# Filter norms and skip terms of a long convolution as rows instead of columns

## The chip, the core and the metric

The kernel runs on one core of a Trainium2 chip. A core has a matrix engine (TensorE, PE; its weight loads are shown apart as PEld), a vector engine (VectorE, DVE), a scalar engine (ScalarE, ACT), GpSimd (POOL), and a queue processor (SyncE, SP) that here issues most of the DMAs. They share an on-chip memory of 128 partitions (SBUF) and the accumulators of TensorE (PSUM). Each engine works through its own list of instructions in order and waits on semaphores for the others. The metric is the device time of one execution in microseconds (us).

## The reference

One layer of an encoder block on x of 2048 positions by 1024 channels, float32: an RMS norm and a projection to a Fourier group (512 channels) and three Hyena groups (3 x 512); a two-dimensional FFT over the Fourier group; an order-2 gated long convolution over the Hyena groups; an output projection, and an MLP. What bears on the change is the filters of the long convolution and how they are used:

```
def implicit_filters(l, w0, b0, w_inner, b_inner, freq, w_out):
    ...                                     # small MLP over the positions: h
    h = (h @ w_out).reshape(l, HYENA_ORDER, N_DIRECTIONS, HYENA_WIDTH)
    h = h * decay[:, None, None, :]
    k = concatenate([h_fwd[:1] + h_bwd[:1], h_fwd[1:], zeros, h_bwd[1:][::-1]])
    return k * lax.rsqrt(jnp.sum(k * k, axis=0, keepdims=True) + EPS)

def fft_long_conv(u, k_freq, d):
    y = jnp.fft.irfft(jnp.fft.rfft(u, n=2 * l) * k_freq)[:l]
    return y + u * d
...
    for n, gate in enumerate((x1, x2)):
        z = gate * fft_long_conv(z, k_freq[:, n], long_d[n])
```

Each of the 2 x 512 filters has 4096 taps and is scaled by one number, the inverse root of its sum of squares plus EPS. The skip term u * d of the convolution is the same as adding d to tap 0 of the scaled filter.

## The kernel before, in words

Products that need full float32 are made of three faster ones (`mm3`, lines 211 to 213, on operands split into a high and a low part by `split`, line 197). The stages follow each other: a first pass of the input projection (to 224 us), a second pass of it with the short convolution (224 to 411), the filters and the Fourier group (411 to 583), then the long convolutions, the output projection and the MLP.

`filters` works on 8 units. Unit i is the channel tile ct = i // 2 (128 channels) and the order n = i % 2 of the convolution. A unit's filter tile `k` has the taps over partitions and columns, the 128 channels inside the columns; tap 0 is partition 0. A unit goes through these parts, spread over a loop of 44 steps, in which several units overlap:

- steps 4u to 4u+3, `generate`: 32 small products (line 596) make a quarter of the taps in a PSUM buffer (`pair`, two buffers in turn, shared with `stage1`), VectorE multiplies it by the decay into `k` (line 601), ScalarE squares it (line 615), GpSimd adds the squares up in `acc` (lines 619 to 622). After the first quarter two taps are added (lines 610 to 612).
- step 4u+5, `normalise` and `scales`: a product sums `acc` over the partitions (`psum_k`, line 627), so that each channel's sum of squares stands in one partition of a 128x1 tile; VectorE adds EPS (`vk`), ScalarE takes the root (line 631), VectorE the reciprocal (line 222) and one Newton step (lines 225 to 227): `sc`. The filter itself is not scaled. Instead tap 0 gets d times the root of the sum (`dk`, line 639, from `vk`, `sc` and `longd`), and the product of the scales of both orders goes into `norms`, which later multiplies the gated input (line 740).
- step 4u+6, `skip`: `dk` is a column, tap 0 of `k` a row over channels. Two products turn the one round and add the other in PSUM (`pdk`, lines 650 and 651), and ScalarE copies the sum back to `k` (line 652). For n = 1 the column of both scales (`both`) is made a diagonal by ScalarE (line 645), a product with ones puts it in all partitions as a row (`pdiag`, line 655), and ScalarE copies it to `norms`.
- from step 4u+7, `stage1` (line 668, transposed out of PSUM by VectorE, line 672) and from 4u+12 `stage2` (line 678, copied by ScalarE, stored by DMA): the filter's spectrum.

`long_d` is loaded as 8 rows of 128, and at the start of `filters` turned into columns (`plongd`, line 556; `longd`, line 557).

The order of TensorE's instructions in this stage is the order of the code, kept by queue-order dependencies (`ordered`, `behind`). The order on the other engines, and of the DMAs on SP's queue, comes from a scheduler, which interleaves all of the program: the steps of the Fourier group (`pf`, lines 508 to 528, and `row`, lines 539 and 540) stand among the first 11 steps, and the weight differences of the MLP (`f`, lines 1484 to 1487, for `second_weights`) among the second pass of the projection.

`rsqrt` has two forms, for a tile of one column and for a wider one:

```
nc.vector.reciprocal(r, s)
if v.shape[1] == 1:
    ...  # 3 tensor_scalar, L225 to L227
nc.vector.tensor_mul(q, r, r)            # L229
nc.vector.tensor_mul(q, q, v)            # L230
nc.vector.tensor_scalar(out=q, in0=q, scalar1=-0.5, scalar2=1.5, ...)  # L231
nc.vector.tensor_mul(q, r, q)            # L232
```

Of the kernel before, what the change touches and what calls it, by code (L numbers as in the profile page):

```python
# [10 lines left out]
F32 = mybir.dt.float32  # L11
# [3 lines left out]
ALU = mybir.AluOpType  # L15

EPS = 1e-5
# [110 lines left out]
P = 128  # L128
# [6 lines left out]
def hybrid_block(ctx: ExitStack, tc: tile.TileContext, A, out):  # L135
    nc = tc.nc
# [36 lines left out]
    def pa(nm):  # L173
        banks["n"] += 1
        pl, tag = (ps, "a") if banks["two"] or banks["n"] % 2 else (banks["other"], "b")
        return pl.tile([P, 512], F32, tag=tag, name=nm, bufs=4)
# [371 lines left out]
            yield  # L548


    def filters(ctx, tp, fp, gp, zp, zzs, norms, emb, wo, e1k, f2, dk8, tabs, fourier_steps):


        longd = fp.tile([P, 16], F32, tag="longd", name="longd")[:, 0:8]
        p = pa("plongd")
        nc.tensor.transpose(p[:, 0:8], dk8, ident[0:8, 0:8])
        nc.scalar.copy(longd, p[:, 0:8])

        class Unit:
            def __init__(self, i):  # L560
# [63 lines left out]
            def normalise(self):  # L624

                p = pa("psum_k")
                ordered(nc.tensor.matmul(p[:, 0:1], lhsT=self.acc[:, 0, :], rhs=ones[:, 0:1], start=True, stop=True))
                self.v = fp.tile([P, 1], F32, tag="vk", name="vk", bufs=2)
                nc.vector.tensor_scalar(out=self.v, in0=p[:, 0:1], scalar1=EPS, scalar2=None, op0=ALU.add)
                self.root = fp.tile([P, 1], F32, tag="sq_k", name="sq_k", bufs=2)  # L630
                nc.scalar.sqrt(self.root, self.v)

            def scales(self):

                v = self.v
                self.sc = rsqrt(v, fp, "k", 8, self.root)
                self.dk = fp.tile([P, 1], F32, tag="dk", name="dk", bufs=2)
                j = 4 * self.n + self.ct
                nc.vector.tensor_scalar(out=self.dk, in0=v, scalar1=self.sc, scalar2=longd[:, j : j + 1], op0=ALU.mult, op1=ALU.mult)
                if self.n:  # L640

                    both = fp.tile([P, 1], F32, tag="both", name="both", bufs=2)
                    nc.vector.tensor_scalar(out=both, in0=self.sc, scalar1=units[self.i - 1].sc, scalar2=None, op0=ALU.mult)
                    self.diag = fp.tile([P, 128], F32, tag="diag", name="diag")
                    nc.scalar.mul(self.diag, ident, both)

            def skip(self):

                p, zero = pa("pdk")[0:1, 0:128], self.k[0:1, :, 0, :]
                ordered(nc.tensor.matmul(p, lhsT=self.dk, rhs=ident, start=True, stop=False))  # L650
                ordered(nc.tensor.matmul(p, lhsT=ones[0:1, 0:1], rhs=zero, start=False, stop=True))
                nc.scalar.copy(zero, p.rearrange("p (c j) -> p c j", c=8))
                if self.n:
                    p = pa("pdiag")
                    ordered(nc.tensor.matmul(p[:, 0:128], lhsT=ones, rhs=self.diag, start=True, stop=True))
                    nc.scalar.copy(norms[:, self.ct], p[:, 0:128])

            def stage1(self, r):
                if r == 0:
# [41 lines left out]
        for step in range(44):  # L701
# [12 lines left out]
                units[u].stage2(2 * q)  # L714
                units[u].stage2(2 * q + 1)
            u, q = divmod(step - 5, 4)
            if 0 <= u < 8 and q < 2:
                (units[u].normalise, units[u].skip)[q]()
            u, k = divmod(step, 4)
            if 0 < step < 32:  # L720
                units[u].generate(k)
# [738 lines left out]
    with pool("ip") as ip, pool("cp1") as cp1:  # L1460
# [67 lines left out]
        e1f, e1k, turn, gy, dk8, e1z, wo, emb, f2 = got  # L1528
    norms = early.enter_context(pool("norms", "right")).tile([P, 4, 128], F32, tag="norms", name="norms")
    with pool("filters") as fp:  # L1530
        zzs, f2h = [], []
        gp = early.enter_context(pool("gk", "right"))
        spx = early.enter_context(ExitStack())
        psum("psd")
        with pool("fourier", "right") as fo:
            ffs.insert(0, load(fo, "ff0", [P, 1, 2, P], A["ff"][:, 0:1]))
            filt = filters(spx, tp, fp, gp, zp, zzs, norms, emb, wo, e1k, f2, dk8, f2h, fourier(fo, uf, e1f, ffs))
            next(filt)
        run(filt)
        psum("psb2")  # L1540
# [73 lines left out]
```

## Time and profile before

| | |
|---|---|
| runs | 2239.90, 2241.47, 2246.95 us; median 2241.47 |
| profiled execution | 2239.05 us, of which the span of the trace 2237.3 |
| mean granted clock of TensorE | 0.996 |
| TensorE busy | 2192.4 us (98%) |
| VectorE busy | 1468.4 us (66%) |
| ScalarE busy | 1072.4 us (48%) |
| GpSimd busy | 762.3 us (34%) |
| stage of the filters | 411 to 583 us |

A row of the timeline gives the start in us, the duration in us, the engine, the line of the kernel, the operation, output<-inputs, tile sizes, how many like instructions were put together (x), and in brackets how long the engine was idle before and what ended that. A group row gives the count, the busy time in us, the mean of one in ns, then the idle time before and what ended most of it. The spans on POOL are rough.

### The profile page before, as it was taken

To read this page: it belongs to the slowest core of one execution; us is meant where nothing else is said; L and a number is where in the kernel's file an instruction comes from. 1 tells how busy PE (TensorE), PEld (TensorE's weight loads), DVE (VectorE), ACT (ScalarE), POOL (GpSimd) and SP (SyncE) were. 2 spreads that over 40 slices of the span, in tenths; PEclk is the share of its full clock that TensorE was granted. 3 is DMA by queue.
4 is the path that set the end of the run, shared out by engine and by line. 5 is a ranking of instruction groups with operands and counts; after the bars stand their busy time and mean duration, and the time that the engine had idled before them with its cause. 6 is when DMAs were issued, how large, how long until landed. Compare 5 with 4: busy or idle time off the path is not lost. (4 is left out here: it accounts for less than half of the span.)

```text
span 2237.3 us, 34489 instructions
## 1 busy us (share of the span) xinstructions
PE 2192.4 (98%) x12881; PEld 1793.3 (80%) x12881; DVE 1468.4 (66%) x2192; ACT 1072.4 (48%) x1783; POOL 762.3 (34%) x576
## 2 busy tenths in 40 slices
PE   8999899999999999999999999999999999999998
PEld 6888778676888778887888878888888888888886
DVE  6998767776788764467444464444476666866667
ACT  6554211355555654546555565555443333533333
POOL 3444323465366511327555446555200000000000
PEclk9999999999999999999999999999999999999999
DMA  8534797569998756586444465444498756866631
GB/s 266 177 134 159 268 335 295 191 218 350 314 306 260 234 161 183 169 265 211 155 156 155 155 238 167 153 146 151 160 381 297 242 188 197 305 194 189 199 111 76
DMA packets 287001, 475.95 MB, mean 213 GB/s; under 512 B 17573, under 2 KB 131439, under 8 KB 282097
## 3 DMA queue, kind: packets, MB, share of 16 engines
q1 hardware_dynamic: 280593, 458.22, 61.5%
q10 hardware_dynamic: 6240, 15.53, 2.1%
q8 instruction: 101, 1.65, 0.3%
q14 instruction: 67, 0.55, 0.1%
HBM read 312.51 MB, written 168.00 MB: 215 GB/s over the span
## 5 line engine op out<-in xcount | busy, mean ns | idle before, releaser
L197 ACT CAST qahm<-ra 128x1024 fp32r<-128x1024 f32 x110 | 115.9, 1053 | 345.0 <-PE p2u L212 171.7
L197 DVE TENSOR_TENSOR qalm<-ra,qahm 128x1024 fp32r<-128x1024 f32 x110 | 134.7, 1224 | 153.4 <-ACT qahm L197 151.7
L1379 POOL TENSOR_TENSOR acc<-acc,gfin 128x512 f32<-128x512 f32 x4 | 5.1, 1282 | 630.2 <-DMA out<-acc 624.4
L212 PE MATMUL pu<-wl,xh 128*128 128x512 f32 x512 | 201.9, 394 | 6.9 <-DVE wl L197 6.5
L211 PE MATMUL pu<-wh,xh 128*128 128x512 f32 x512 | 204.9, 400 | 2.6 <-ACT wh L201 2.6
L213 PE MATMUL pu<-wh,xl 128*128 128x512 f32 x512 | 201.8, 394 | 2.7 <-DVE xl L197 2.7
L212 PE MATMUL p2u<-qblm,qahm 128*128 128x512 f32 x504 | 196.1, 389 | 0.0
L211 PE MATMUL p2u<-qbhm,qahm 128*128 128x512 f32 x504 | 195.8, 389 | 0.0
L213 PE MATMUL p2u<-qbhm,qalm 128*128 128x512 f32 x504 | 195.8, 389 | 0.0
L197 DVE TENSOR_TENSOR qblm<-rb,qbhm 128x1024 fp32r<-128x1024 f32 x110 | 134.0, 1218 | 2.2 <-ACT qbhm L197 2.2
L421 POOL TENSOR_TENSOR acc<-acc,cw 128x512 f32<-128x512 f32 x45 | 60.9, 1354 | 197.5 <-DVE acc L398 194.3
L212 PEld LDWEIGHTS pu<-wl,xh 128*128 128x128 f32 x512 | 97.4, 190 | 28.8 <-DVE wl L197 6.9
L197 ACT CAST ahm<-s 128x512 fp32r<-128x512 f32 x120 | 74.4, 621 | 94.1 <-PE p1v L212 54.8
L197 ACT CAST qbhm<-rb 128x1024 fp32r<-128x1024 f32 x110 | 115.3, 1048 | 4.4 <-DMA rb<-in_w_fc 2.9
L213 PEld LDWEIGHTS pu<-wh,xl 128*128 128x128 f32 x512 | 97.2, 190 | 24.4 <-DVE xl L197 4.1
L211 PEld LDWEIGHTS pu<-wh,xh 128*128 128x128 f32 x512 | 97.4, 190 | 23.8 <-ACT wh L201 3.5
L197 POOL TENSOR_TENSOR alm<-W,ahm 128x512 fp32r<-128x512 f32 x60 | 83.3, 1390 | 86.8 <-ACT ahm L197 86.8
L211 PEld LDWEIGHTS p2u<-qbhm,qahm 128*128 128x128 f32 x504 | 94.6, 188 | 20.1 <-issue 0.3
L213 PEld LDWEIGHTS p2u<-qbhm,qalm 128*128 128x128 f32 x504 | 94.6, 188 | 19.8
L212 PEld LDWEIGHTS p2u<-qblm,qahm 128*128 128x128 f32 x504 | 94.6, 188 | 19.5
L1155 DVE TENSOR_TENSOR c<-p1v,ku 128x512 f32<-128x512 f32 x64 | 44.2, 690 | 89.9 <-ACT ku L1225 51.2
L197 POOL TENSOR_TENSOR alm<-s,ahm 128x512 fp32r<-128x512 f32 x60 | 92.2, 1537 | 29.6 <-ACT ahm L197 29.6
(379 smaller groups left out, 6148.9 us busy)
## 6 DMA issues: line engine op xcount, KB each, us to landing
ks<-spec SPq DMA_DIRECT2D x64, 512.0 KB
W<-in_w_fc SPq DMA_DIRECT2D x64, 512.0 KB
rb<-td SPq DMA_DIRECT2D x64, 512.0 KB
ra<-a1m SPq DMA_DIRECT2D x56, 512.0 KB
ra<-a0m SPq DMA_DIRECT2D x54, 512.0 KB
rb<-in_w_fc SPq DMA_DIRECT2D x46, 512.0 KB
f<-in_w_fc SPq DMA_DIRECT2D x16, 1024.0 KB
td<-f SPq DMA_DIRECT2D x16, 1024.0 KB
```

The lines of the kernel that those rows point to most:

```text
L197: return nc.scalar.copy(hi, src), eng.tensor_sub(lo, src, hi)
L211: a = nc.tensor.matmul(o, lhsT=lh, rhs=rh, start=start, stop=False, skip_group_check=more)
L212: nc.tensor.matmul(o, lhsT=lh, rhs=rl, start=False, stop=False, skip_group_check=more)
L213: return a, nc.tensor.matmul(o, lhsT=ll, rhs=rh, start=False, stop=stop, skip_group_check=more)
L421: nc.gpsimd.tensor_add(m1, m1, cw[:, 3, :])
L1155: read["DVE"] = nc.vector.tensor_add(c, p, other)
L1379: nc.gpsimd.tensor_mul(acc[i][:, c], acc[i][:, c], gfin[:, c])
```

## The change

The sums stand as rows from the start. `psum_k` becomes a product with ones on the other side: it puts every channel's sum in all 128 partitions, 128 columns wide. EPS, root, reciprocal and Newton step are done on these 128x128 tiles (the wide form of `rsqrt`). Tap 0 of `k` is in partition 0, where the row of sums stands too, so `dk` is made there by two products of 1x128 and added to `k` by VectorE; `norms` is the product of two 128x128 tiles. `skip`, `both`, `diag`, `pdk`, `pdiag`, `longd` and `plongd` go. `long_d` is loaded as one row per unit in one partition, at the start of `filters`.

```diff
-    def filters(ctx, tp, fp, gp, zp, zzs, norms, emb, wo, e1k, f2, dk8, tabs, fourier_steps):
-        longd = fp.tile([P, 16], F32, tag="longd", name="longd")[:, 0:8]
-        p = pa("plongd")
-        nc.tensor.transpose(p[:, 0:8], dk8, ident[0:8, 0:8])
-        nc.scalar.copy(longd, p[:, 0:8])
+    def filters(ctx, tp, fp, gp, zp, zzs, norms, emb, wo, e1k, f2, tabs, fourier_steps):
+        dk8 = load(fp, "dk8", [1, 8, 128], A["long_d"])
...
             def normalise(self):
                 p = pa("psum_k")
-                ordered(nc.tensor.matmul(p[:, 0:1], lhsT=self.acc[:, 0, :], rhs=ones[:, 0:1], start=True, stop=True))
-                self.v = fp.tile([P, 1], F32, tag="vk", name="vk", bufs=2)
-                nc.vector.tensor_scalar(out=self.v, in0=p[:, 0:1], scalar1=EPS, scalar2=None, op0=ALU.add)
-                self.root = fp.tile([P, 1], F32, tag="sq_k", name="sq_k", bufs=2)
+                ordered(nc.tensor.matmul(p[:, 0:128], lhsT=ones, rhs=self.acc[:, 0, :], start=True, stop=True))
+                self.v = fp.tile([P, 128], F32, tag="vk", name="vk")
+                nc.vector.tensor_scalar(out=self.v, in0=p[:, 0:128], scalar1=EPS, scalar2=None, op0=ALU.add)
+                self.root = fp.tile([P, 128], F32, tag="sq_k", name="sq_k")
                 nc.scalar.sqrt(self.root, self.v)
             def scales(self):
-                v = self.v
-                self.sc = rsqrt(v, fp, "k", 8, self.root)
-                self.dk = fp.tile([P, 1], F32, tag="dk", name="dk", bufs=2)
-                j = 4 * self.n + self.ct
-                nc.vector.tensor_scalar(out=self.dk, in0=v, scalar1=self.sc, scalar2=longd[:, j : j + 1], op0=ALU.mult, op1=ALU.mult)
+                self.sc = rsqrt(self.v, fp, "k", 2, self.root)
+                dk, zero = self.root[0:1], self.k[0:1, :, 0, :]
+                nc.vector.tensor_mul(dk, self.v[0:1], self.sc[0:1])
+                nc.vector.tensor_mul(dk, dk, dk8[:, self.i])
+                nc.vector.tensor_add(zero, zero, dk.rearrange("p (c j) -> p c j", c=8))
                 if self.n:
-                    both = fp.tile([P, 1], F32, tag="both", name="both", bufs=2)
-                    nc.vector.tensor_scalar(out=both, in0=self.sc, scalar1=units[self.i - 1].sc, scalar2=None, op0=ALU.mult)
-                    self.diag = fp.tile([P, 128], F32, tag="diag", name="diag")
-                    nc.scalar.mul(self.diag, ident, both)
-            def skip(self):
-                p, zero = pa("pdk")[0:1, 0:128], self.k[0:1, :, 0, :]
-                ordered(nc.tensor.matmul(p, lhsT=self.dk, rhs=ident, start=True, stop=False))
-                ordered(nc.tensor.matmul(p, lhsT=ones[0:1, 0:1], rhs=zero, start=False, stop=True))
-                nc.scalar.copy(zero, p.rearrange("p (c j) -> p c j", c=8))
-                if self.n:
-                    p = pa("pdiag")
-                    ordered(nc.tensor.matmul(p[:, 0:128], lhsT=ones, rhs=self.diag, start=True, stop=True))
-                    nc.scalar.copy(norms[:, self.ct], p[:, 0:128])
+                    nc.vector.tensor_mul(norms[:, self.ct], self.sc, units[self.i - 1].sc)
...
-            if 0 <= u < 8 and q < 2:
-                (units[u].normalise, units[u].skip)[q]()
+            if 0 <= u < 8 and q == 0:
+                units[u].normalise()
...
-                got.append(cpool.tile([8, 128], F32, tag="dk8", name="dk8"))
-                for n in range(2):
-                    nc.sync.dma_start(got[-1][4 * n : 4 * n + 4, :], A["long_d"].rearrange("a (c n) j -> n (a c) j", n=2)[n])
```

Three places show what stands on the engines now. In the changed kernel the lines behind `rsqrt` have other numbers (601 becomes 598, 672 becomes 654, 668 becomes 650, 678 becomes 660, 596 becomes 593, 1484 to 1487 become 1466 to 1469). First VectorE (DVE), unit 4 (n = 0), from its sum to the second product by the decay behind it; before:

```order
L629 TENSOR_SCALAR vk<-psum_k 128x1
L222 RECIPROCAL rc_k<-sq_k 128x1
L225 TENSOR_SCALAR nw_k<-rc_k,vk 128x1
L226 TENSOR_SCALAR nw_k<-nw_k 128x1
L227 TENSOR_SCALAR nw_k<-nw_k,rc_k 128x1
L639 TENSOR_SCALAR dk<-vk,nw_k,longd 128x1
L601 TENSOR_TENSOR k<-pk,dec 128x8x8x16
L672 STREAM_TRANSPOSE Gk<-pk_5171 128x8x2x32 x2
L601 TENSOR_TENSOR k<-pk,dec_4723 128x8x8x16
```

And on the same engine at the same place in the changed kernel:

```order
L626 TENSOR_SCALAR vk<-psum_k 128x128
L222 RECIPROCAL rc_k<-sq_k 128x128
L229 TENSOR_TENSOR nw_k<-rc_k 128x128
L230 TENSOR_TENSOR nw_k<-nw_k,vk 128x128
L231 TENSOR_SCALAR nw_k<-nw_k 128x128
L598 TENSOR_TENSOR k<-pk,dec 128x8x8x16
L232 TENSOR_TENSOR nw_k<-rc_k,nw_k 128x128
L634 TENSOR_TENSOR sq_k<-vk,nw_k 1x128
L635 TENSOR_TENSOR sq_k<-sq_k,dk_3611 1x128
L654 STREAM_TRANSPOSE Gk<-pk_5146 128x8x2x32 x2
L636 TENSOR_TENSOR k<-k,sq_k 1x8x16
L598 TENSOR_TENSOR k<-pk,dec_4706 128x8x8x16
```

The operations became 128 columns wide, and three more of them stand ahead of the transpose; the add into tap 0 stands behind it. With n = 1 the product for `norms` (line 638) stands ahead of the transpose too. Second, TensorE (PE) at the same place, before:

```order
L627 MATMUL psum_k<-ones,acc 128x1
L596 MATMUL pk<-wo,emb 32x128 x32
L668 MATMUL pk_5171<-k,e1k 32x512 x8
L678 MATMUL pk_5190<-Gk,f_2585 128x128 x4
L678 MATMUL pk_5197<-Gk,f_2585 128x128 x4
L650 MATMUL pdk<-ident,dk 1x128
L651 MATMUL pdk<-k,ones 1x128
L596 MATMUL pk<-wo,emb 32x128 x32
L668 MATMUL pk_5248<-k,e1k 32x512 x8
```

And TensorE in the changed kernel:

```order
L624 MATMUL psum_k<-acc,ones 128x128
L593 MATMUL pk<-wo,emb 32x128 x32
L650 MATMUL pk_5146<-k,e1k 32x512 x8
L660 MATMUL pk_5167<-Gk,f_2582 128x128 x4
L660 MATMUL pk_5174<-Gk,f_2582 128x128 x4
L593 MATMUL pk<-wo,emb 32x128 x32
L650 MATMUL pk_5221<-k,e1k 32x512 x8
```

The two `pdk` products are gone; the order is the same otherwise. Third, VectorE in one of the blocks of the second projection pass (`xl` is the low part of a block of x that TensorE multiplies by, `f` the weight differences), before:

```order
L398 SCALAR_TENSOR_TENSOR m_3134<-pu_3103,nw_s,cw_2366 128x512
L197 TENSOR_TENSOR xl<-xc,xh 128x1024
L417 TENSOR_TENSOR acc<-acc,m_3134 128x512
L1484 TENSOR_TENSOR f_2585<-f_2585 128x512
L1485 TENSOR_TENSOR f_2585<-f_2585 128x512
```

And VectorE in the same block of the changed kernel:

```order
L398 SCALAR_TENSOR_TENSOR m_3131<-pu_3100,nw_s,cw_2366 128x512
L1466 TENSOR_TENSOR f_2582<-f_2582 128x512
L417 TENSOR_TENSOR acc<-acc,m_3131 128x512
L1467 TENSOR_TENSOR f_2582<-f_2582 128x512
L197 TENSOR_TENSOR xl<-xc,xh 128x1024
L1468 TENSOR_TENSOR f_2582<-f_2582 128x512
L1469 TENSOR_TENSOR f_2582<-f_2582 128x512
```

Two weight differences stand ahead of the split of x here; in another block it is the other way round. On SP's queue, with one load fewer, some loads of this pass stand up to 15 places earlier.

More of the change, by code (lines that the diff above doesn't have):

```diff
@@ L1527, in hybrid_block @@
         run(project(ip, fx, (None, cp1), (-1, 0), uf), tables())
-        e1f, e1k, turn, gy, dk8, e1z, wo, emb, f2 = got
+        e1f, e1k, turn, gy, e1z, wo, emb, f2 = got
     norms = early.enter_context(pool("norms", "right")).tile([P, 4, 128], F32, tag="norms", name="norms")
@@ L1536, in hybrid_block @@
             ffs.insert(0, load(fo, "ff0", [P, 1, 2, P], A["ff"][:, 0:1]))
-            filt = filters(spx, tp, fp, gp, zp, zzs, norms, emb, wo, e1k, f2, dk8, f2h, fourier(fo, uf, e1f, ffs))
+            filt = filters(spx, tp, fp, gp, zp, zzs, norms, emb, wo, e1k, f2, f2h, fourier(fo, uf, e1f, ffs))
             next(filt)
```

## The prediction

> **What bounds the kernel now.** I read the page's first part, then busy time by engine in the stretches around the filters, then the timeline of the two engines that the change touches.
>
> ```profile
> span 2237.3 us, 34489 instructions
> PE 2192.4 (98%) x12881; PEld 1793.3 (80%) x12881; DVE 1468.4 (66%) x2192; ACT 1072.4 (48%) x1783; POOL 762.3 (34%) x576
> 435.00:461.00 26.00, 24.12 (x557) 18.30 (x555) 18.94 (x43) 17.12 (x54) 14.46 (x14) 1.00 0.54 187
> 461.00:553.00 92.00, 89.03 (x2049) 65.12 (x2050) 61.44 (x108) 49.03 (x104) 54.27 (x49) 1.00 0.81 301
> 553.00:583.00 30.00, 29.65 (x299) 22.28 (x299) 19.92 (x37) 13.69 (x27) 3.52 (x5) 1.00 0.87 326
> ```
>
> The columns of the last three rows are the length, then busy PE, PEld, DVE, ACT and POOL. TensorE is busy 98% of the span and 97% in the middle of the filters (89.03 of 92), where the granted clock is 1.00; VectorE (DVE) is busy two thirds there. On these averages, whatever TensorE no longer issues is gained and VectorE has room. The timeline shows where that fails. TensorE in two steps after a sum (unit 4, n = 0), with the start, duration and operation in each row, and two steps of unit 3 (n = 1):
>
> ```profile
> 503.22 1.16 PE L596 MATMUL pk<-wo,emb 64*32 64x128 f32 x64
> 504.12 1.12 PE L668 MATMUL pk<-k,e1k 64*32 64x512 f32 x16
> 505.17 2.05 PE L678 MATMUL pk<-Gk,f 128*128 128x128 f32 x16
> 507.15 0.38 PE L650 MATMUL pdk<-ident,dk 128*1 128x128 f32 x2
> 507.76 1.16 PE L596 MATMUL pk<-wo,emb 64*32 64x128 f32 x64
> 508.66 1.12 PE L668 MATMUL pk<-k,e1k 64*32 64x512 f32 x16
> 511.69 1.07 PE L596 MATMUL pk<-wo,emb 64*32 64x128 f32 x59
> ...
> 486.25 1.16 PE L596 MATMUL pk<-wo,emb 64*32 64x128 f32 x64
> 490.90 0.49 PE L655 MATMUL pdiag<-diag,ones 128*128 128x128 f32 x2
> 495.25 1.16 PE L596 MATMUL pk<-wo,emb 64*32 64x128 f32 x64
> ```
>
> A step is generate, stage1, stage2. Undisturbed it takes 3.93 us (507.76 to 511.69). The step with the two pdk products takes 4.54 (503.22 to 507.76): they cost 0.61. With n = 1 two steps take 9.00 (486.25 to 495.25) against 7.86 undisturbed: pdk and pdiag cost up to 1.14. VectorE in the same stretch:
>
> ```profile
> 503.76 0.12 DVE L629 TENSOR_SCALAR vk<-psum_k 128x1 f32<-128x1 f32 x1
> 504.24 0.16 DVE L222 RECIPROCAL rc_k<-sq_k 128x1 f32<-128x1 f32 x1 [0.36 <-ACT sq_k L631]
> 504.44 0.27 DVE L225 TENSOR_SCALAR nw_k<-rc_k,vk 128x1 f32<-128x1 f32 x1
> 504.75 0.15 DVE L226 TENSOR_SCALAR nw_k<-nw_k 128x1 f32<-128x1 f32 x1
> 504.94 0.21 DVE L227 TENSOR_SCALAR nw_k<-nw_k,rc_k 128x1 f32<-128x1 f32 x1
> 505.19 0.27 DVE L639 TENSOR_SCALAR dk<-vk,nw_k,longd 128x1 f32<-128x1 f32 x1
> 505.38 1.22 DVE L601 TENSOR_TENSOR k<-pk,dec 128x1024 f32<-128x1024 f32 x1
> 506.51 1.31 DVE L672 STREAM_TRANSPOSE Gk<-pk 128x512 f32<-128x512 f32 x2
> 508.97 1.23 DVE L601 TENSOR_TENSOR k<-pk,dec 128x1024 f32<-128x1024 f32 x1 [1.16 <-PE pk L596]
> 461.32 0.94 PE L596 MATMUL pk<-wo,emb 64*32 64x128 f32 x48 [0.48 <-DVE k L601]
> ```
>
> generate and stage1 share two pair buffers in PSUM, so TensorE may not begin the second stage1 (508.66) before VectorE has transposed the first one out (506.51 to 507.8): 0.85 us of slack. The last row is such a wait where slack was used up. The scalar chain stands ahead of that transpose in VectorE's queue, so widening it by more than 0.85 us makes TensorE wait there, however idle VectorE is afterwards (1.16 us before 508.97). That wait decides, not the share of busy time.
>
> **The change part by part.** TensorE's saving: 4 x 0.61 (n = 0) + 4 x 1.14 (n = 1), so at most 7.0 us. The sum's product now has 128 columns, not 1; two records of the 128-column f32 pdiag take 0.49 us against 0.38 for pdk, so 0 to 0.1, taken as nothing. plongd and its copy go out of a time in which TensorE waits for something else, ScalarE's L480: nothing.
>
> ```profile
> 411.00 1.16 PE L596 MATMUL pk<-wo,emb 64*32 64x128 f32 x64 [0.62 <-ACT uf L480]
> ```
>
> One load in place of two is nothing on a queue that isn't waited for.
>
> VectorE's additions need the price of 128 columns. Rows that bear on it (count, then busy time and mean ns):
>
> ```profile
> L222 DVE RECIPROCAL rc_k<-sq_k 128x1 f32<-128x1 f32 x8 | 1.3, 161 | 2.1 <-ACT sq_k L631 2.1
> L226 DVE TENSOR_SCALAR nw_k<-nw_k 128x1 f32<-128x1 f32 x8 | 1.2, 153 | 0.3
> L540 DVE TENSOR_TENSOR row<-pf,sb 128x124 f32<-128x124 f32 x1 | 0.3, 277 | 0.0
> L305 DVE TENSOR_SCALAR arg<-arg 128x512 f32<-128x512 f32 x12 | 5.1, 424 | 0.3
> L615 ACT ACTIVATE sqr<-k 128x512 f32<-128x512 f32 x56 | 32.8, 625 | 39.4 <-DVE k L601 36.7 <-POOL acc L619 2.5
> ```
>
> A product of two 128-wide tiles: 0.28 (L540, 124 wide), 0.31 with the gap to the next. One scalar operation 128 wide: 0.15 + 127 x (0.424 - 0.153)/511 = 0.22. The square root on ScalarE: 0.21 + 127 x (0.625 - 0.21)/511 = 0.31. The unknown is the reciprocal 128 wide. From below it costs what the 124-wide product does, 0.28. From above: for one element it takes 8 ns longer than a scalar operation (161 and 153); were that per element, 128 would take 0.16 + 127 x 0.008 = 1.18. I take 1.18, since a cost of dividing that shows at all with one element is likelier to repeat than not.
> The Trainium skill, "VectorE: DVE Perf Modes", section "First, the fixed hardware budget", says that reciprocal is an iterative divide with a repeat count of 8, where other operations deliver one result per cycle at 0.96 GHz; that gives an estimate of 128 x 8/0.96 GHz = 1.07 us, and the sum would be some 0.1 us less per unit. The 8 ns extra of one element agrees with it; no row here is wide.
>
> Unit 4 again (in the order that the changed queue has): vk 503.76 to 504.04; root to 504.47; reciprocal 504.50 to 505.68; two products to 506.30; scalar to 506.55; generate's product L601 506.5 instead of 505.38, to 507.72; three products to 508.53; transposes 508.45 instead of 506.51, to 509.76. The second stage1 starts at 509.80 instead of 508.66, and the step after it at 512.83 instead of 511.69: **+1.14**, the saved pdk already in it. For n = 1 the norms' product adds 0.31 more ahead of the transpose: two steps take 9.92 instead of 9.00, **+0.92**. With the cheap reciprocal both are 0.90 less: +0.24 and +0.02.
>
> The new add into k's row 0 and the other products read two SBUF operands, as this add does:
>
> ```profile
> 468.40 0.46 POOL L622 TENSOR_TENSOR acc<-acc 128x128 f32<-128x128 f32 x1
> 468.44 0.56 DVE L611 TENSOR_TENSOR k<-k,lag 1x128 f32<-1x128 f32 x1 [0.36 <-ACT lag L610]
> 501.98 0.28 DVE L611 TENSOR_TENSOR k<-k,lag 1x128 f32<-1x128 f32 x1 [0.37 <-ACT lag L610]
> 455.41 0.15 DVE L222 RECIPROCAL rc_k<-sq_k 128x1 f32<-128x1 f32 x1
> 458.74 2.64 POOL L619 TENSOR_TENSOR acc<-acc,sqr 128x512 f32<-128x512 f32 x2 [4.93 <-ACT sqr L615]
> 460.06 1.22 DVE L601 TENSOR_TENSOR k<-pk,dec 128x1024 f32<-128x1024 f32 x1
> 541.59 0.38 PE L596 MATMUL pk<-wo,emb 64*32 64x128 f32 x5 [1.64 <-issue]
> ```
>
> Beside a GpSimd add the same instruction took 0.56, else 0.28: it ended when GpSimd's did. So a new operation can wait for one GpSimd add, up to 1.32 (2.64 for two).
> The Trainium skill, "SBUF — State Buffer", section "Terms", says that the two engines share a port pair as an exclusive lock held for the whole instruction; the 0.56 agrees.
>
> Unit 1 is walked from the row at 455.41: reciprocal 1.21 with gap, two products 0.62, L601 1.15, scalar and product 0.56, transposes 1.26, three products 0.93, the two row products of the other transform 0.66, the add 0.31; the next L601 starts at 462.1 instead of 460.06. TensorE waits on that one already (461.32 above), so +2.05 is all on the path. GpSimd adds run back to back from 458.74, so 0 to 1.32 of waiting is added; I take 0.75: **+2.8**. Unit 0 lies in a stretch with more idle time on both engines (24.12 and 18.94 of 26): between 0 and one GpSimd add, 1.3; **+0.7**. Unit 7 has no generate behind it: between -1.1 (its skip saved) and +1.1; **+0.4**, since its add into k lies just ahead of the stage1 that reads it.
>
> Sum: 0.7 + 2.8 + 3 x 1.14 (units 2, 4, 6) + 2 x 0.92 (units 3, 5) + 0.4 = +9.1. In 529 to 546 TensorE also stops for nothing the profile names (1.64 in the row above); lateness may hide there, 0 to 1.6, taken as 0.6. **+8.5 us.** The profiled execution took 2239.05 (its span and 1.75 around it), so it would come to 2247.5; the median of the runs is 2241.47, 2.4 above it, and I predict on that: **2250.0**.
>
> **The rivals.** *B, a cheap reciprocal.* It costs 0.28, like other operations. For it: 8 ns in 160 is near what such means scatter by. Six units at 0.90 less, and unit 1 likewise: +8.5 - 6.3 = +2.2, **2243.7**.
>
> *C, the other side: faster.* VectorE's additions fit its idle time (61.44 of 92 busy) and TensorE keeps its whole 7.0: **2234.5**. It decides if the chain ahead of the transpose grows by less than the 0.85 of slack at 508.66. Against it: in the walk it grows by 1.94 (506.51 to 508.45), and by 1.04 even with the cheap reciprocal.
>
> *D, another order in the second projection pass.* The queue of VectorE changes there too: splits that TensorE waits for stand ahead of or behind the weight differences.
>
> ```profile
> 300.34 0.19 PEld L213 LDWEIGHTS pu<-wh,xl 128*128 128x128 f32 x1 [2.14 <-DVE xl L197]
> 345.09 0.19 PEld L213 LDWEIGHTS pu<-wh,xl 128*128 128x128 f32 x1 [1.36 <-DVE xl L197]
> ```
>
> These waits, 3.5 us together, may vanish or come twice. **2253.5** or **2246.5**.
>
> **How the numbers follow.** A, the forecast, 0.50, its own range 2246 to 2256 (lock waits all or none, unit 7's and the stall's bounds); B 0.22; C 0.10; D 0.08 on each side; 0.02 for what I don't see. About 0.3%, 6.7 us, is what a measurement of this kernel can tell from no change, so slower begins at 2248.2 and faster at 2234.8. Slower: 0.41 of A, 0.01 of B, 0.08 of D, 0.01 of the rest = 0.51. Faster: half of C and a part of the rest = 0.06. Same: the other 0.43. The range leaves out C and the ends of A and D: 2238 to 2257.
>
> **What would show it.** The reciprocal's row 128 wide near 1.2 us (B: 0.3); two steps after a sum 9.6 us with n = 0, with TensorE's wait put down to the transpose's or generate's tile; generate after unit 1's sum late by 2 to 3 us; the new add longer than 0.28 wherever GpSimd runs; busy TensorE in the middle stretch falling below 97% of it while the stretch grows. The forecast is wrong if TensorE shows no new wait behind these transposes, or if the stretch from 224 to 411 moves by more than 2 us.

## The result and the profile after

The changed kernel takes 2253.82 us (median of 7 runs, 2247.86 to 2259.15), the kernel before 2241.47 (7 runs, 2236.91 to 2246.95). The ratio is 1.0063, 95% interval 1.0052 to 1.0074: 14.1 us slower (0.0063 x 2241.47; the two medians are 12.4 apart). The same kernel measured a second time against other runs of before gave 1.0054 (1.0042 to 1.0066). The traced execution took 2252.42 us, its span 2250.6: 13.3 more than the span of before.

First the page of the changed kernel, then its rows of busy time by stretch (length, busy PE, PEld, DVE, ACT, POOL; behind them the granted clock, the DMA share and GB/s), and last the second projection pass in the kernel before:

```profile
span 2250.6 us, 34406 instructions
PE 2190.1 (97%) x12840; PEld 1793.6 (80%) x12840; DVE 1487.4 (66%) x2216; ACT 1070.6 (48%) x1766; POOL 756.6 (34%) x576
224.00:411.00 187.00, 175.27 (x748) 143.62 (x747) 127.28 (x156) 31.80 (x52) 52.81 (x35) 0.96 0.79 283
461.00:553.00 92.00, 80.07 (x1910) 58.27 (x1910) 71.82 (x121) 45.24 (x93) 50.92 (x45) 1.00 0.73 263
...
224.00:411.00 187.00, 177.21 (x768) 145.20 (x768) 131.88 (x158) 32.86 (x53) 58.53 (x39) 0.98 0.82 290
```

TensorE was busy 89.03 of the middle 92 us and is now busy 80.07; VectorE went from 61.44 to 71.82. TensorE has fewer instructions and more idle time. Where it waits, by what released it (total, times, longest), between 436 and 600, of the changed kernel and then two rows of the kernel before:

```profile
PE pk L593 <- DVE k L598: 4.8, 4, 2.9
PE pk L650 <- DVE Gk L654: 3.5, 4, 1.0
PE pk L650 <- DVE k L636: 2.4, 2, 1.9
...
PE pk L596 <- issue: 3.0, 3, 1.6
PE pk L596 <- DVE k L601: 0.5, 1, 0.5
```

In the kernel before, the first of these was 0.5 us once, and the other two were not there; its 3.0 us behind "issue" are idle time that the profile puts down to no engine, which is called a hole below. These are the waits of the forecast: the decay product, the transposes out of the pair buffers, and the new add into tap 0. They sum to 10.7 us.

The starts of the eight filter sums (`psum_k`) on TensorE are good marks, since each unit has one. Read off the timelines of both kernels:

| | first sum | 1 to 2 | 2 to 3 | 3 to 4 | 4 to 5 | 5 to 6 | 6 to 7 | 7 to 8 | 8th to the end |
|---|---|---|---|---|---|---|---|---|---|
| before | 435.92 | 18.18 | 15.38 | 16.56 | 16.97 | 16.44 | 19.21 | 18.02 | 1680.6 |
| changed | 440.17 | 18.46 | 18.97 | 17.59 | 17.38 | 20.04 | 18.26 | 18.99 | 1680.7 |
| difference | +4.25 | +0.28 | +3.59 | +1.03 | +0.41 | +3.60 | -0.95 | +0.97 | +0.1 |
| forecast | 0 | +0.7 | +2.8 | +1.14 | +0.92 | +1.14 | +0.92 | +1.14 | +0.4 |

From the first sum to the end the kernel lost 9.0 us where 8.5 were forecast (9.1 less 0.6 hidden). It lost 4.25 more ahead of the first sum, in the second projection pass. From the first to the eighth sum, before and then changed:

```profile
435.92:556.68 120.76, 116.22 (x2637) 85.53 (x2637) 81.16 (x150) 67.14 (x159) 71.39 (x64) 1.00 0.76 275
440.17:569.86 129.69, 113.79 (x2602) 84.40 (x2603) 99.61 (x171) 65.97 (x146) 71.27 (x64) 0.99 0.72 255
```

TensorE's idle time grew from 4.5 to 15.9 us, more than its busy time fell. The clock of 0.99 is one stretch of 3.41 us at a granted clock of 0.50 (from 556.48), which costs 1.7 us and for which the forecast had no term.

Unit 4 of the changed kernel, TensorE and then VectorE, answers the walk of the prediction:

```profile
512.88 1.16 PE L593 MATMUL pk<-wo,emb 64*32 64x128 f32 x64
517.29 1.16 PE L593 MATMUL pk<-wo,emb 64*32 64x128 f32 x64 [0.38 <-DVE k L598]
519.44 1.09 PE L650 MATMUL pk<-k,e1k 64*32 64x512 f32 x16 [0.99 <-DVE Gk L654]
522.44 1.16 PE L593 MATMUL pk<-wo,emb 64*32 64x128 f32 x64
...
514.24 0.95 DVE L222 RECIPROCAL rc_k<-sq_k 128x128 f32<-128x128 f32 x1 [0.38 <-ACT sq_k L628]
516.02 1.22 DVE L598 TENSOR_TENSOR k<-pk,dec 128x1024 f32<-128x1024 f32 x1
517.99 1.30 DVE L654 STREAM_TRANSPOSE Gk<-pk 128x512 f32<-128x512 f32 x2
519.22 0.30 DVE L636 TENSOR_TENSOR k<-k,sq_k 1x128 f32<-1x128 f32 x1
```

From the generate behind the sum the second stage1 starts 6.56 us later (519.44 - 512.88) and the step after it 9.56 (522.44 - 512.88). The forecast had 6.58 (509.80 - 503.22) and 9.61 (512.83 - 503.22), the kernel before 5.44 and 8.47. The transposes end at 519.3, and stage1 starts at 519.44: that is the wait.

The new operations as groups between 435 and 600 (count, busy us, mean ns), and the second pass of the changed kernel where TensorE waits for a split of x, with the instructions ahead of that split on VectorE and the stretch behind it:

```profile
L222 DVE RECIPROCAL rc_k<-sq_k 128x128 f32<-128x128 f32 x8 | 7.6, 950 | 2.2 <-ACT sq_k L628 2.2
L229 DVE TENSOR_TENSOR nw_k<-rc_k 128x128 f32<-128x128 f32 x8 | 3.4, 431 | 0.3
L232 DVE TENSOR_TENSOR nw_k<-rc_k,nw_k 128x128 f32<-128x128 f32 x8 | 2.3, 282 | 0.0
L636 DVE TENSOR_TENSOR k<-k,sq_k 1x128 f32<-1x128 f32 x8 | 4.3, 540 | 0.1
...
304.62 0.69 DVE L1466 TENSOR_TENSOR f<-f 128x512 f32<-128x512 f32 x1 [6.47 <-DMA f<-in_w_fc]
307.20 0.69 DVE L1467 TENSOR_TENSOR f<-f 128x512 f32<-128x512 f32 x1
309.50 0.68 DVE L1468 TENSOR_TENSOR f<-f 128x512 f32<-128x512 f32 x1
310.10 1.21 DVE L197 TENSOR_TENSOR xl<-xc,xh 128x1024 fp32r<-128x1024 f32 x1
311.37 0.79 PE L213 MATMUL pu<-wh,xl 128*128 128x512 f32 x1 [3.05 <-DVE xl L197]
311.00:314.00 3.00, 2.63 (x6) 2.15 (x7) 2.30 (x4) 1.62 (x2) 0.00 (x0) 0.50 0.66 198
314.00:317.00 3.00, 3.00 (x8) 2.31 (x7) 2.94 (x5) 0.00 (x0) 0.82 (x1) 0.50 0.90 367
```

The reciprocal 128 wide takes 0.95 us, between the two ends of the forecast and near the upper one. In the second pass the split of x stands behind three weight differences, the first of which waited 6.47 us for its weights; TensorE was idle 3.05 us, and then ran at half its clock for over 6 us. In the kernel before, the waits there were shorter (1.72 and 0.94 us) and no such stretch followed.

### The profile page after: what moved, and what is told of

The parts are those of the page before. It is cut to its first block, busy times and chain, and to the rows that moved or that the text cites. A ratio compares the mean times of both kernels' runs of the same rounds, so it can differ in the third digit from the quotient of the medians.

```text
span 2250.6 us, 34406 instructions
## 1 busy us (share of the span) xinstructions
PE 2190.1 (97%) x12840; PEld 1793.6 (80%) x12840; DVE 1487.4 (66%) x2216; ACT 1070.6 (48%) x1766; POOL 756.6 (34%) x576
## 4 chain that ended last, share of the span: by engine, by line
PE 85%; DVE 5%; DMA 4%; ACT 3%; issue 1%; POOL 1%; SPq 0%; ACTq 0%; DVEq 0%; POOLq 0%
PE p2u L212 5%; PE p2u L211 5%; PE p2u L213 5%; PE p1u L211 5%; PE p1u L212 5%; PE p1u L213 5%; PE pu L212 4%; PE pu L213 4%; PE pu L211 4%; PE p2v L211 3%; PE p2v L212 3%; PE p2v L213 3%; PE pz L772 2%; PE p1v L211 2%; PE p1v L213 2%; PE p1v L212 2%
## 5 line engine op out<-in xcount | busy, mean ns | idle before, releaser
L213 PEld LDWEIGHTS p2u<-qbhm,qalm 128*128 128x128 f32 x504 | 94.6, 188 | 19.6
L211 PE MATMUL p1u<-bm,ahm 128*128 128x512 f32 x252 | 99.5, 395 | 5.6 <-ACT ku L1207 3.9
```

The costliest lines, as they stand in the source:

```text
L211: a = nc.tensor.matmul(o, lhsT=lh, rhs=rh, start=start, stop=False, skip_group_check=more)
L213: return a, nc.tensor.matmul(o, lhsT=ll, rhs=rh, start=False, stop=stop, skip_group_check=more)
```

## The experiments

All were measured beside runs of the kernel before on the same chip; ratios are to those runs.

**The order of the second pass, put back (rows in the filters).** This is called the first run below. Only the two old loads are issued again, into a tile that nothing reads; this puts the second pass on SP, VectorE, ScalarE, TensorE and GpSimd back in the order of before.

```diff
                 got.append(load(cpool, "gy", [P, 8], A["g_y"]))
+                unused = cpool.tile([8, 128], F32, tag="dk8", name="unused")
+                for n in range(2):
+                    nc.sync.dma_start(unused[4 * n : 4 * n + 4, :], A["long_d"].rearrange(...)[n])
```

> The change, with the two loads of long_d as 8x128 kept where they were in the second projection pass (into a tile that nothing reads). This brings back the order of before on every queue of that pass; the filters stay as changed. Theory (order): the 4.3 us that the changed kernel has lost before its first filter sum (440.17 against 435.9) come from that order, so the first sum is back at 435.9 +- 0.5, no stretch of the second pass has a granted clock of 0.5, and the time is 9 us over before, ratio 1.0040. Rival (scatter): the 4.3 us are a difference between executions; the ratio stays at 1.0063.

Measured: 1.0040 (1.0026 to 1.0054), 2248.31 against 2238.98 us. That is 9.0 us (0.0040 x 2241), where the prediction had 8.5 for the filters. Its first sum is at 435.07, a little ahead of what was expected. But the second pass does have a stretch at half the clock here too, behind a shorter wait, and the filters have another behind the wait of unit 1:

```profile
299.06 0.50 PE L213 MATMUL pu<-wh,xl 128*128 128x512 f32 x1 [2.08 <-DVE xl L197]
299.70:303.00 3.30, 3.30 (x9) 2.54 (x8) 1.99 (x3) 1.33 (x2) 0.00 (x0) 0.50 0.77 219
464.38 0.89 PE L593 MATMUL pk<-wo,emb 64*32 64x128 f32 x24 [2.87 <-DVE k L598]
463.60:470.20 6.60, 5.82 (x90) 4.16 (x91) 4.49 (x6) 2.42 (x5) 4.13 (x4) 0.50 0.17 64
```

**The order of the second pass, changed alone (columns in the filters).**

```diff
                 got.append(cpool.tile([8, 128], F32, tag="dk8", name="dk8"))
-                for n in range(2):
-                    nc.sync.dma_start(got[-1][4 * n : 4 * n + 4, :], A["long_d"].rearrange(...)[n])
...
     def filters(...):
+        for n in range(2):
+            nc.sync.dma_start(dk8[4 * n : 4 * n + 4, :], A["long_d"].rearrange(...)[n])
```

> The kernel before, with only the two loads of long_d taken out of the second projection pass (issued at the start of the filters' code instead). The queues of that pass get the order of the changed kernel; the filters stay as before. Theory (order): TensorE waits about 3 us for a split of x near 311, the granted clock falls to 0.5 there for about 6 us, and the time is 4.3 us over before, ratio 1.0019. Rival (scatter): 1.000.

Measured: 1.0041 (1.0028 to 1.0054), so 9.2 us, twice what was expected. The trace has the loss ahead of the filters: its first sum is at 445.65, and from the first to the eighth sum it takes 121.44 us, as before (120.76). Two waits of TensorE in it, and the stretch behind the first (the second has one too):

```profile
315.12 0.50 PE L213 MATMUL pu<-wh,xl 128*128 128x512 f32 x1 [3.46 <-DVE xl L197]
342.35 0.50 PE L213 MATMUL pu<-wh,xl 128*128 128x512 f32 x1 [3.57 <-DVE xl L197]
316.18:319.58 3.40, 3.40 (x10) 2.63 (x9) 3.08 (x5) 0.91 (x1) 0.00 (x0) 0.50 0.85 209
```

**The changed kernel a second time.** No edit.

> The changed kernel once more, for a second trace of its second projection pass. Theory (order): the first filter sum again at 440 or later, with a wait of 3 us or more for a split of x and a stretch at a granted clock of about 0.5 behind it; eight traces with the order of before have it between 432.9 and 439.0. Rival (scatter): it can fall anywhere in 433 to 440, and the ratio falls to that of the first run of this study, 1.0040.

Measured: 1.0054 (1.0042 to 1.0066), first sum at 442.42, with this wait, and this stretch that begins near its end:

```profile
338.12 0.79 PE L213 MATMUL pu<-wh,xl 128*128 128x512 f32 x1 [4.61 <-DVE xl L197]
336.95:343.70 6.75, 5.58 (x13) 4.42 (x14) 6.71 (x8) 1.24 (x2) 3.42 (x2) 0.50 0.79 263
```

The long wait is at another block than in the first trace, so it is not one place that is slow; the new order lets such waits grow past 3 us, here and there. TensorE's waits for a split between 280 and 400 sum to 5.2, 6.0 and 8.2 us in the three traces with the new order, and to 0.8 to 3.8 in the eleven with the order of before. Those three have the first sum at 440.17, 442.42 and 445.65, the eleven (the kernel before, and ten of the kernels in this study) between 432.89 and 439.85, 436.7 in the mean. The order costs something in each comparison at hand: with rows 1.0063 or 1.0054 against 1.0040 (5.2 or 3.1 us), with columns 1.0041 against 1 (9.2 us). Only the last is far outside the noise; with rows each difference is known to about 4 us. The two do not agree on the size, and the traces differ by 7 us with one order, so the size stays at 3 to 9 us.

**The chain moved behind the transposes.** Made from the first run of the study; `tap0`, up to the add into k, is called a step after `scales`, and `both` a step after that. `flipped` is the last transpose of the step.

```diff
             def scales(self):
-                self.sc = rsqrt(self.v, fp, "k", 2, self.root)
...
+                behind([nc.vector.reciprocal(r, self.root)], flipped)
+                behind([nc.vector.tensor_mul(q, r, r)], flipped)
+            def tap0(self):
+                behind([nc.vector.tensor_mul(q, q, v)], flipped)
...
+            def both(self):
+                if self.n:
+                    behind([nc.vector.tensor_mul(norms[:, self.ct], self.sc, units[self.i - 1].sc)], flipped)
```

> As the first run of this study, with the same operations on rows, but on VectorE the reciprocal and the first product behind the transposes of their step, the rest up to the add into tap 0 behind the transposes of the next step, the product for norms a step later. Theory (place in the queue): TensorE's new waits on transposes and decay products of units 2 to 7 (0.9 to 1.0 us each) go, the 7.0 us of products saved appear, less 1 to 3 us in units 0 and 1: 4 to 6 us faster than before, ratio 0.9973 to 0.9982. Rival (load): the new VectorE work costs what it costs wherever it stands, by its length and by waits beside GpSimd: +5 to +9 us, 1.0022 to 1.0040.

Measured: 1.0109 (1.0096 to 1.0123), 24 us slower than before and 15 slower than the first run. Both theories fell; the place does matter, but this one is worse. Its waits of TensorE between 436 and 600, and a chain of VectorE with the GpSimd adds beside it:

```profile
PE pk L664 <- DVE k L647: 19.6, 8, 4.8
...
527.01 1.31 DVE L668 STREAM_TRANSPOSE Gk<-pk 128x512 f32<-128x512 f32 x2
528.23 1.16 DVE L641 TENSOR_TENSOR nw_k<-nw_k,vk 128x128 f32<-128x128 f32 x1
529.42 1.24 DVE L642 TENSOR_SCALAR nw_k<-nw_k 128x128 f32<-128x128 f32 x1
530.69 0.29 DVE L643 TENSOR_TENSOR nw_k<-rc_k,nw_k 128x128 f32<-128x128 f32 x1
...
527.96 2.62 POOL L616 TENSOR_TENSOR acc<-acc,sqr 128x512 f32<-128x512 f32 x2 [1.28 <-ACT sqr L612]
```

Behind the transposes stand GpSimd's two adds of each step. The product L641 ended when the first did, and the scalar operation L642, which has one tensor operand, ended when the second did (1.24 us instead of 0.23). The add into tap 0 (L647) came late, and stage1, which reads the whole of tap 0, waited for it at all 8 units. Five of these waits are followed by a stretch at half the clock: the mean granted clock between 436 and 600 is 0.93, where the first run has 0.98.

**The same without GpSimd's adds.**

```diff
-                    if sq is not self.acc:
-                        nc.gpsimd.tensor_add(self.acc, self.acc, sq)
-                if k == 3:
...
+                    if sq is not self.acc and k == 3 and q == 1:
+                        summed[:] = [nc.gpsimd.tensor_add(self.acc[:, 0, :], self.acc[:, 0, :], sq[:, 0, :])]
```

> The third run of this study (the chain behind the transposes) without GpSimd's sums of squares, but for one 128x128 add for each unit; the scales are wrong numbers. In the third run TensorE waited 19.6 us in 8 waits for the add into tap 0. Theory (GpSimd): two instructions of the chain took 1.16 and 1.24 us beside GpSimd adds, not 0.29 and 0.23; without these the chain ends 1.8 us earlier and the filters lose about 8 x 1.7 = 13 us: ratio 1.005. Rival (the chain is too long for its place): at most 4 us less than the third run, 1.009.

Measured: 1.0034 (1.0021 to 1.0046), 16.8 us less than the run with them (0.0075 x 2241). The waits for the add into tap 0 fell from 19.6 to 8.0:

```profile
PE pk L661 <- DVE k L644: 8.0, 7, 2.9
```

So GpSimd's adds made most of that loss, and the chain's own length the rest. Part of it came by the clock: with the waits shorter, the granted clock between 436 and 600 is 0.98, not 0.93, which is 8.5 us less lost to half clock (3.4 for 11.9).

**The reciprocal left out.**

```diff
-        nc.vector.reciprocal(r, s)
+        if nm == "k":
+            nc.vector.tensor_scalar(out=r, in0=s, scalar1=0.0, scalar2=0.05, op0=ALU.mult, op1=ALU.add)
+        else:
+            nc.vector.reciprocal(r, s)
```

> As the first run of this study, with the 128x128 reciprocal of each unit replaced by one scalar operation of the same size (0.22 us instead of 0.95); the scales are wrong numbers. Theory (length of the chain ahead of the transpose): 0.73 us less in about 6 units, so 4.4 us less than the first run: +4.6 us over before, ratio 1.0020. Rival (GpSimd: the waits of two-operand additions set the loss, not the reciprocal): less than 1.5 us of change, ratio 1.0034 to 1.0040.

Measured: 1.0026 (1.0016 to 1.0035), 3.1 us under the first run, between the two theories and, with intervals of 0.0014 and 0.0010, clear of neither. From the first to the eighth sum the traces give 130.97 us with the reciprocal and 127.16 without, 3.8 less, against 4.4 expected and under 1.5 by the rival; the one without lost 1.7 us more to half clock there, so the wait itself shrank by more. The reciprocal is 3 to 4 us of the loss, and not the whole of it.

**TensorE's products put back.** Made from the first run; `skip` is called at its old place.

```diff
+            def skip(self):
+                p = pa("pdk")[0:1, 0:128]
+                ordered(nc.tensor.matmul(p, lhsT=ones[:, 0:1], rhs=ident, start=True, stop=False))
+                ordered(nc.tensor.matmul(p, lhsT=ones[0:1, 0:1], rhs=ident[0:1, :], start=False, stop=True))
+                if self.n:
+                    p = pa("pdiag")
+                    ordered(nc.tensor.matmul(p[:, 0:128], lhsT=ones, rhs=ident, start=True, stop=True))
```

> The first run of this study (rows in the filters, order of before in the second pass) with the products of skip put back on TensorE at their old places: 16 pdk and 4 pdiag products that read constant tiles and whose results nobody reads. Theory (TensorE waits for VectorE behind each sum, so that its saving is not on the path there): the products fill waits of 0.9 to 1.0 us; at most 2 us more than the first run, ratio 1.0040 to 1.0049. Rival (the saving of 7 us is had, and VectorE's chain costs 16): 7 us more than the first run, ratio 1.0071.

Measured: 1.0039 (1.0026 to 1.0052), where the first run had 1.0040; the rival's 1.0071 is ruled out. The products that the change saves cost nothing that shows (give or take 4 us) when they are put back: in the changed kernel TensorE would have waited in that time.

**TensorE's products left out of the kernel before.** `copies` has the two copies of `skip` alone, from tiles in SBUF.

```diff
-                (units[u].normalise, units[u].skip)[q]()
+                (units[u].normalise, units[u].copies)[q]()
```

> The kernel before (scales in columns) without the products of skip; ScalarE copies other values of the same size to the same places, so the skip terms and norms are wrong numbers. This is TensorE's saving alone, with no new work on VectorE. By the rows of before: 4 x 0.61 + 4 x 1.14 = 7.0 us, ratio 0.9969. Rival (TensorE is held by something else in these steps, so that a hole in its list is not a gain): within 2 us of before, 0.9991 to 1.0009.

Measured: 0.9997 (0.9988 to 1.0006): -0.7 us, where 7.0 were expected. So the saving is hardly a gain even without any new work on VectorE. Up to the fifth sum this trace is 2.8 us shorter than before (64.30 against 67.09 from the first sum); then comes this:

```profile
514.05 1.12 PE L674 MATMUL pk<-k,e1k 64*32 64x512 f32 x16 [3.72 <-issue]
510.00:515.00 5.00, 1.28 (x41) 0.28 (x22) 1.67 (x3) 1.47 (x3) 3.68 (x4) 1.00 1.01 406
515.00:518.40 3.40, 3.40 (x23) 3.30 (x16) 1.31 (x2) 0.59 (x1) 0.00 (x0) 0.50 1.02 423
432.89:552.77 119.88, 111.63 (x2602) 84.82 (x2602) 81.20 (x150) 68.35 (x159) 71.17 (x64) 0.99 0.77 275
```

TensorE stood for 3.72 us for nothing that the profile names, and its clock fell to half for 3.41 us behind that. Such holes sum to 5.7 us here, to 3.0 in the kernel before, to 5.1 in the changed one. The last row is the stretch from the first to the eighth sum: TensorE is busy 4.6 us less than before, and 6.3 less but for the half clock, and idle 3.7 us more (8.2 against 4.5), so most of what the products saved in this trace went into idle time and half clock.

**A version with less ahead of tap 0.** Rows, the order of before in the second pass; d times the root goes straight into tap 0, and one inverse root of the product of both sums makes the norms, for n = 1 alone, a part (`scale`) in each of four later steps.

```diff
-                self.sc = rsqrt(self.v, fp, "k", 2, self.root)
-                dk, zero = self.root[0:1], self.k[0:1, :, 0, :]
-                nc.vector.tensor_mul(dk, self.v[0:1], self.sc[0:1])
-                nc.vector.tensor_mul(dk, dk, dk8[:, self.i])
+                dk, zero = dk8[:, self.i], self.k[0:1, :, 0, :]
+                nc.vector.tensor_mul(dk, self.root[0:1], dk)
                 nc.vector.tensor_add(zero, zero, dk.rearrange("p (c j) -> p c j", c=8))
...
+            def scale(self, part):
+                a, b = units[self.i - 1], self
+                if part == 0:
+                    behind([nc.vector.tensor_mul(a.root, a.root, b.root)], flipped)
+                    behind([nc.vector.tensor_mul(a.v, a.v, b.v)], flipped)
+                elif part == 1:
+                    behind([nc.vector.reciprocal(b.root, a.root)], flipped)
...
```

> Rows as in the changed kernel, order of before in the second pass, with less in the chain that tap 0 waits for: the skip term is d times the root itself (one product and the add, no reciprocal), and the norms are one inverse root of the product of both orders' sums, for n = 1 alone, one or two instructions behind the transposes of each of four steps. Theory (the chain ahead of the transpose decides): its additions fall from 1.94 us to less than the slack of 0.85, TensorE's products stay saved: 5 to 7 us faster than before, ratio 0.9969 to 0.9978. Rival (any 128-wide work on VectorE meets GpSimd's adds and stops TensorE): not faster, 0.9995 or above.

Measured: 0.9995 (0.9985 to 1.0005), 2239.79 us. It is 10 us faster than the first run, so what the filters lost by was the work ahead of tap 0 and of the transposes. But it does not beat the kernel before, where 5 to 7 us were expected: as in the run without the products of skip, the saved products are not a gain.

**Fewer bytes in the filters.** To see whether full DMA engines make the holes: the kernel before, then without the products of skip, then the version above, each with three spectra stored once (the second copies get other numbers in the first projection pass).

```diff
-                    n = 1 if self.i in SINGLE else 2
+                    n = 1 if self.i in SINGLE + (2, 4, 6) else 2
...
     def filters(...):
+        for i in (2, 4, 6):
+            nc.sync.dma_start(kd[i // 2][0][1].rearrange("p s x -> (p s) x"), A["f2k"].rearrange("p f c -> p (f c)"))
```

> The kernel before with fewer bytes in the filters: the spectra of units 2, 4 and 6 are stored once, not twice (3 x 2 MB less between about 480 and 560); so that something stands there, their second copies are filled with other numbers in the first projection pass, and the result is wrong. This run is the base for the next two. Theory (TensorE's holes that the profile names nothing for, 3.0 us here and 5.7 without the products of skip, come from full DMA engines): holes under 1 us, so 2 us less from the first to the last filter sum (120.76 in the kernel before). Rival (they have nothing to do with the transfers): 3 us of holes as before.

> The run before this one (fewer bytes in the filters) with the products of skip left out too, as in the run of the full traffic. Theory (full DMA engines took back the saving): with light traffic the products' time is gained, 5 to 7 us less than the run before this one, and holes under 1 us. Rival (the saving is not on the path for another reason): at most 2 us less, as with full traffic.

> Fewer bytes in the filters as in the run of light traffic, with rows as in the run of the root into tap 0. Theory (full DMA engines): this kernel's saving shows too, 4 to 6 us less than the run of light traffic. Rival (the new work on VectorE is what it loses by): within 2 us of the run of light traffic.

Measured: 1.0014 (1.0004 to 1.0025), 0.9979 (0.9969 to 0.9989) and 0.9995 (0.9986 to 1.0004). Beside the run of light traffic, leaving out the products gains 0.0035, 7.8 us (give or take 3.3, from both intervals), and the version with the root 0.0019, 4.3 us (give or take 3.1), which is near what the theory said of the times. But the base became 3 us slower instead of 2 faster, and that makes a part of both: beside the kernel before, lighter traffic took the run without the products from 0.9997 to 0.9979 (4.0 us, give or take 3.0) and left the version with the root at 0.9995. The holes do not fit the theory either. They are 3.9, 4.7 and 5.5 us in these three, no fewer than with full traffic, where under 1 us was expected. The DMA share between 500 and 550 fell only from 0.95 in the kernel before to 0.78 to 0.80. So full DMA engines are not shown to be the cause.

What the holes end with can be read in the traces. Beside the kernel's transfers the profile lists a DMA queue of kind "instruction" (q8), whose packets of 16 KB come 24 times between 436 and 600 in the changed kernel. In the 14 traces TensorE has 47 holes of 0.3 us or more in that stretch. Of these, 46 end 1.20 to 1.58 us after such a packet has landed, and one 0.91 us; of its 99 other waits of that length, 11 end at that distance. The packet in the hole of 3.72 us landed at 512.59, and TensorE went on at 514.05. So in the holes TensorE most likely waits for its own instructions. The packets take about 1 us there as elsewhere; why these come too late, and whether lighter traffic can bring them sooner, is not shown.

## Why the prediction was right, and where it was off

**The bound** was read rightly: the slack of 0.85 us ahead of stage1 decided, not the shares of busy time. The new waits stand at the tiles named (transposes, decay product, tap 0), and putting the products back cost nothing that shows.

**Unit 4's walk** held to 0.05 us (6.56 and 9.56 against 6.58 and 9.61), partly by errors that cancel: the reciprocal took 0.95, not 1.18, while vk came at 0.74 after the generate instead of 0.54, behind a lag add that took 0.56 beside GpSimd. The rule of the Trainium skill ("VectorE: DVE Perf Modes", section "First, the fixed hardware budget") gave an estimate of 1.07; the measured 0.95 is nearer to it than to the 1.18 from one-element rows. It is (0.95 - 0.16)/127 = 6.2 ns per element, not 8, and the measurement decides.

**Unit 1** lost 3.59, not 2.8. The end of its chain in the changed kernel, with GpSimd and then TensorE beside it:

```profile
465.25 0.67 DVE L634 TENSOR_TENSOR sq_k<-vk,nw_k 1x128 f32<-1x128 f32 x1
466.05 1.35 DVE L635 TENSOR_TENSOR sq_k<-sq_k,dk 1x128 f32<-1x128 f32 x1
464.51 2.75 POOL L616 TENSOR_TENSOR acc<-acc,sqr 128x512 f32<-128x512 f32 x2 [5.30 <-ACT sqr L612]
469.44 1.16 PE L593 MATMUL pk<-wo,emb 64*32 64x128 f32 x64 [2.87 <-DVE k L598]
```

Two products took 0.67 and 1.35 us, where 0.28 is usual: 1.46 us of waiting beside GpSimd's adds, where 0.75 was taken. In the first run and in the second trace of the changed kernel this part lost 6.0 and 5.4 us (21.39 and 20.76 against 15.38), 3.4 and 1.7 of it by half clock. **Unit 2** came as forecast (1.03 for 1.14). **Unit 6** came near it (0.97 for 1.14) by luck: its part has a hole of 1.77 us and the stretch at half clock in the changed kernel, and a hole of 1.64 before; in the two other traces just named it took 17.18 and 17.22, 0.8 less than before. **Unit 0** lost 0.28 for 0.7, **unit 3** 0.41 for 0.92. **Unit 4** (3.60 for 1.14) has a hole of 2.16 in the changed kernel. **Unit 5** (-0.95 for 0.92) has holes of 0.81 before and of 0.42 and 0.71 in the changed kernel; besides, two groups of products took 1.2 us longer before than their like in the prediction's rows (2.01 for 1.12 and 2.36 for 2.05). **Unit 7** lost 0.1 for 0.4. So the sum is better than its parts.

**Rival B** (cheap reciprocal) fell with 0.95 us. **Rival C**, that TensorE keeps 7.0 us, fell twice: VectorE's chain did pass the slack, and the 7.0 us are no gain even alone (-0.7).

**Rival D** was the step that failed in the forecast: the second pass was taken at nothing, with 0.08 for a loss there, and the changed order cost 3 to 9 us. By the prediction's own sign (that stretch moving by more than 2 us) the forecast was wrong here: it moved by 4.25. The sum for the filters alone gives 2250.0 and was met (1.0040, so 2250.4); the whole 2253.8 is forecast plus D, 2253.5. The rows quoted for D had both waits, but the prediction took them to vanish or double; it had no term for the clock, here or in the filters. That the filters were met without one is partly luck: of the 10.2 us that the first run lost between its first and its eighth sum (130.97 against 120.76), 3.4 are half clock.

## What to carry to other kernels

Widening a scalar chain from one column to 128 costs by its place: read how long the next engine can go on before it needs what stands behind the chain in the queue, and price the chain against that slack. A few matmuls saved in a step are a gain only if nothing else sets that step's end; leave them out alone and measure. A wait of some 2 us on TensorE can cost 1.7 us or more again by the clock, so read the granted clock behind each. Compare the order of every queue even for a part of the program that the change does not touch: dropping a load moved splits and weight differences in another stage, and in the trace that was about a third of the loss (4.25 of 13.3 us).

## What was not expected of the hardware

- Between 224 and 600 every stretch at a granted clock of 0.50 lasted 3.41 us or two or three times that, so it costs 1.7 us or more on top of the wait. Each came behind an idle time of TensorE of 1.77 us or more, or began in it. All 14 traces have one near 233, behind a wait of 6.5 us; in the second pass, waits of 1.81, 2.08 and 3.46 us were each followed by one stretch of 3.41 us, 3.05 and 4.61 by 6.83 us. Not every such wait is: 1.72 in the kernel before and 2.87 (unit 1) in the changed one were followed by 1.00. The Trainium skill, "TensorE: Matmul & The Clock Gate", section "What's actually happening", has the clock fall to half after an idle window of about 3.4 us; here 1.77 was enough once, and 1.81 and 1.85 in others.
- A one-operand scalar operation of 128x128 on VectorE also waited for a GpSimd add (1.24 us instead of 0.23), not only products of two SBUF tiles.
- TensorE's unnamed holes lie mostly between 495 and 570, in the stage of its smallest products, and sum to 1.1 to 5.7 us in the traces here. Nearly all end about 1.4 us after an instruction packet of 16 KB has landed.
